# The order of the seven products in an FFN's second projection: 1, 5 | 7, 6, 2, 3 | 4 in place of 1 | 2 | 5, 6, 7, 3 | 4

## The chip, the cores and the metric

The kernel runs on one core of a Trainium2 chip. A core has five engines with instruction streams of their own: TensorE (PE; its weight loads are listed apart as PEld), VectorE (DVE), ScalarE (ACT), GpSimd (POOL) and SyncE (SP), and 16 DMA engines that serve transfers issued by SP, ACT and POOL. The metric is the device time of one execution in microseconds, the median over several runs.

## The reference

Two layers of an encoder over 512 tokens of width 1024. A layer is half an FFN, a mixer, and half an FFN; a last RMSNorm follows. All weights are float32.

```python
def swiglu(x, w_in, w_out):
    gu = x @ w_in
    g, u = jnp.split(gu, 2, axis=-1)
    return (jax.nn.silu(g) * u) @ w_out
...
    for l in range(L):
        x = x + 0.5 * swiglu(rms_norm(x, ffn1_norm[l]), ffn1_w_in[l], ffn1_w_out[l])
        x = x + mixer(rms_norm(x, mix_norm[l]), mix_w_in[l], mix_gate_bias[l], na_rpb[l],
                      na_w_out[l], f_w_out[l], mix_w_o[l])
        x = x + 0.5 * swiglu(rms_norm(x, ffn2_norm[l]), ffn2_w_in[l], ffn2_w_out[l])
    return rms_norm(x, final_norm)
```

So there are four FFNs. The change concerns the product with `w_out` (2816 x 1024) in each of them, called the second projection or the output stage below.

## The kernel before

**A matrix product as seven.** The kernel halves both operands of its large products in both directions and forms seven products of half size in place of eight (Strassen's scheme in Winograd's form). With a, b, c, d the quarters of the weight matrix (upper and lower left, upper and lower right) and A11, A12, A21, A22 those of the activations, the output stage computes

| product | activations | weights |
|---|---|---|
| 1 | A11 | -a |
| 2 | A21 | b |
| 5 | A11 - A12 | c + d |
| 6 | A11 - A12 + A22 | a + c + d |
| 7 | A12 - A22 | a + c |
| 3 | A22 | a + b + c + d |
| 4 | A21 - (A11 - A12 + A22) | d |

(with activations transposed, so that "rows" of the code's `part(h, j, c)` are h for the halves of the 2816 features and j for the halves of the tokens). Product 6 is added onto product 1 in PSUM, and product 4 onto product 7. Results go into x, which stays in SBUF as float32, by `update` (L817 to L820): one DVE instruction for each of the two 128-token blocks, x = x ± 0.25 · PSUM. Product 1 is read into x before product 6 is added to it, and once more after each further step that needs the sum.

**Chunks.** The 1408 features of a half are cut into three chunks of 3, 4 and 4 tiles of 128 (`CHUNK`, L47). A product of one chunk takes two granules of weights, of two 128 x 512 tiles each (in the first chunk the second granule has one tile); each granule is used for two blocks of tokens.

**Precision.** Each float32 operand is split into a high and a low part of a shorter type, and a tile of a product is three matmuls: high x high, high x low, low x high (L539, L540, L542; 128 x 512 each). The high part is an ACT copy, the low part a DVE subtraction. For weights these are L205 or L210 (`whi`) and L206 or L213 (`wlo`), with three buffers each; for activations L350 and L351 (`c1h`, `c1l` and so on, by the number of the product). The differences and sums of the activations are made in place by DVE (`comb`, L814).

**Weights.** `stage_items` (L220) writes out the whole list of granules in the order in which products use them; `strassen` (L226) makes the items of one product after the other. `Raw.load` (L150) issues a plain load from SP (L155) into one of nine `raw` tiles of an FFN stage, and, where the item has a `plus`, an accumulating DMA from POOL that adds a second block of weights onto the tile (L165). An item with `add` gets its second block by its own plain load and a DVE addition (`summed`, L182). An item with `then` gets a further block by an accumulating DMA once the item is split (L215); with `dma=True` (the last chunk of the last FFN) this takes the place of a DVE addition. Before, product 5 uses a tile d onto which c is accumulated, product 6 adds a to the same tile (DVE), product 3 adds b to it (DVE), and product 7 has a tile of its own, c with a accumulated. `Stream.next` (L334) lets the splits run two granules ahead of PE, and the loads eight items ahead in the instruction order (`FETCH`), as far as the nine tiles allow.

**Order.** In `stage_ffn` (L663) the second projection is a list `steps` (L822) of (product, chunk): product 1 for the three chunks, product 2 for the three, then 5, 6, 7, 3 of the first chunk, of the second and of the third, then product 4 for the three. `make(i)` builds the activation operand of step i, up to three steps ahead. The loop from L996 runs the products and puts around them, by step: the turned blocks of the FFN's inner activations (`joined`, after steps 3 and 5; the transposing DMA is L381), the updates of x, the squares for the next norm (ACT, L413), and the transposed quarters of x for the next stage (`nxt.quad`, L437 to L456: eight PE transposes L451, four ACT copies L454, one high part L455, one low part on DVE L456). Quarter (0, 0) is placed after step 6, which is product 5's first chunk; (1, 1) and (0, 1) after product 4's first chunk. In the last FFN (`late`) there are no quarters, and the final norm is woven in. 

**Banks.** The PSUM pool has eight tiles of 128 x 512 (L110). A product's output takes a pair. `ps` holds the pairs o1, o2, o5, o7, o3 while they are in use; product 6 uses o1, product 4 o7.

**Who decides the order.** Semaphores and the instruction order on each engine are set by the framework's scheduler: it takes the ready instruction that comes first in the program, by a model of the durations, so that DVE may run differences (L814) well ahead of the place where the code has them. Blocks under `manual_schedule` keep their order on the engines named.

Of the kernel before, what the change touches and what calls it, by code (L numbers as in the profile page):

```python
# [31 lines left out]
AHEAD = 2  # L32
ORDER = (1, 5, 2, 6, 7, 3, 4)
FIRST = (1, 2, 5, 6, 7, 3, 4)
FETCH = 8
UNIT = (0, 1, 4, 5)
KEYS = ((0, 6), (2, 5), (2, 4), (1, 6))
# [61 lines left out]
def encoder_kernel(  # L99
# [120 lines left out]
    def stage_items():  # L220
        items, st = [], 0

        def add(*a, **k):
            items.append(Item(*a, stage=st, **k))

        def strassen(s, name, idx, sizes, order, dma=False, behind=None, on_chip=False):  # L226
            def key(q, g):
                return (s, name(q), idx, g) if g < 2 else (s, "h" + q, idx, 0)

            r = {}  # L230
            for q, q2 in (("a", None), ("b", None), ("c", "a"), ("d", "c")):
                plus = q2 and not (on_chip and q == "c")
                r[q] = [Raw(key(q, g), n, key(q2, g) if plus else None) for g, n in enumerate(sizes)]
            d2 = [Raw(key("d", g), n) for g, n in enumerate(sizes)]
            at = [(m, g) for m in order for g in range(len(sizes))]
            if len(sizes) == 3:
                at.remove((2, 2))
                at.insert(at.index((7, 2)), (2, 2))
            for m, g in at:
                a, b, c, d = [r[q][g] for q in "abcd"]  # L240
                if m == 1:
                    add(a, neg=True)
                elif m == 2:
                    add(b)
                elif m == 3:
                    add(d, None if dma else b)
                elif m == 4:
                    add(d2[g])
                elif m == 5:
                    add(d)  # L250
                elif m == 6:
                    add(d, a, then=b.key if dma else None)
                else:
                    add(c, a if on_chip else None)
                for key in (behind or {}).get(m, ()) if g == len(sizes) - 1 else ():
                    add(Raw(key))

        def out_sizes(c):
            return (1024, 512) if c == 0 else (1024, 1024)

        def ffn(s):
            first = not items
            if first:
                for g in range(4):
                    add(Raw((s, "cl", g)), parts=2 if g < 2 else 1, pieces=2 if g == 0 else 1)
            for j in range(NB):
                order = (1, 2, 5, 6, 7, 3, 4) if first and j == 0 else (1, 5, 6, 2, 7, 3, 4)
                strassen(s, lambda q: q, j, (1024,) * (2 if first or j else 3), order)
            for order in ((1,), (2,), (5, 6, 7, 3), (4,)):
                for c in range(3):  # L270
                    summed = s == (L - 1, 2) and c == 2
                    strassen(s, lambda q: "o" + q, c, out_sizes(c), order, summed)

        for l in range(L):
            ffn((l, 1))
            st += 1
            s = (l, 0)
            two = (1024, 1024)
            qk = [(s, "qk", g) for g in range(8)]
            strassen(s, lambda q: "u" + q, 0, two, (1, 5, 6, 2, 3, 7, 4), True, behind={5: qk[0:1], 6: qk[1:2], 2: qk[2:3], 3: qk[3:4], 7: qk[4:5]})  # L280
            for key in qk[5:]:
                add(Raw(key))
            halves = [((s, "f", 2 * i), (s, "f", 2 * i + 1)) for i in range(2)]
            even = [Raw(t1, plus=t2) for t1, t2 in halves]
            for raw in even:
                add(raw)
            for raw, (_, t2) in zip(even, halves):
                add(raw, Raw(t2), twice=True)
            st += 1
            for g in range(2):  # L290
                add(Raw((s, "n", 0, g)))
            st += 1
            for i in range(2):
                strassen(s, lambda q: "g" + q, i, two, ORDER if i else FIRST, True, on_chip=False)
            for g in range(2):
                add(Raw((s, "n", 1, g)))
            strassen(s, lambda q: "w" + q, 0, two, ORDER, True)
            ffn((l, 2))
        return items
# [363 lines left out]
    def stage_ffn(norm, nxt, late):  # L663
# [140 lines left out]
        def part(h, j, c):  # L804
            return at[h, j, c][:, 0 : len(CHUNK[0][c]), :]
# [7 lines left out]
        def comb(dst, in0, in1, op):  # L813
            V.tensor_tensor(dst, in0, in1, op)  # L814
            return dst
# [3 lines left out]
                v = x[:, 2 * j + b, i * T : (i + 1) * T]  # L819
                V.scalar_tensor_tensor(v, ps[b], 0.25 * sign, v, ALU.mult, ALU.add)  # L820

        steps = []  # L822
        for c in range(3):
            steps.append((1, c, lambda c=c: part(0, 0, c)))
        for c in range(3):
            steps.append((2, c, lambda c=c: part(1, 0, c)))
        for c in range(3):
            steps.append((5, c, lambda c=c: comb(part(0, 0, c), part(0, 0, c), part(0, 1, c), ALU.subtract)))
            steps.append((6, c, lambda c=c: comb(part(0, 0, c), part(0, 0, c), part(1, 1, c), ALU.add)))
            steps.append((7, c, lambda c=c: comb(part(0, 1, c), part(0, 1, c), part(1, 1, c), ALU.subtract)))  # L830
            steps.append((3, c, lambda c=c: part(1, 1, c)))
        for c in range(3):
            steps.append((4, c, lambda c=c: fourth(c)))
        made = {}
        apart_by = set()

        def fourth(c):
            if c not in apart_by:
                comb(part(1, 0, c), part(1, 0, c), part(0, 0, c), ALU.subtract)
                apart_by.add(c)  # L840
            return part(1, 0, c)

        def make(i):
            if i < len(steps) and i not in made:
                m, c, f = steps[i]
                made[i] = hl(f(), c, f"c{m}")

        def two(settle):

# [143 lines left out]
        if late or nxt.mix:  # L993
            tc.keep_in_program_order(S.activation(small("sq", 1), ones, AF.Sqrt))
        ps = {}
        for i, (m, c, _) in enumerate(steps):  # L996
            make(i)
            if i:
                make(i + 1)
# [24 lines left out]
                    else:  # L1024
                        nxt.quad(0, 1)
            make(i + 2)
            if i == 6 and not late:
                nxt.quad(0, 0)
            if m == 4 and c == (0 if late else 1):
                update(ps[1], 1, 0, 1)  # L1030
# [7 lines left out]
            if m == 4 and c == 1 and late:  # L1038
                for _ in ready:
                    pass  # L1040
            if c < 2:
                continue
            if m == 1:
                update(ps[1], 0, 0, -1)
            elif m == 2:
                update(ps[2], 0, 0, 1)
                nxt.squares(0, 0)
            elif m == 5:
                update(ps[5], 0, 1, 1)
                update(ps[5], 1, 1, -1)  # L1050
            elif m == 6:
                if late:
                    make(i + 3)
                    fourth(2)
                update(ps[1], 1, 1, 1)
            elif m == 7:
                if late:
                    make(i + 3)
                update(ps[7], 1, 1, 1)
                nxt.squares(1, 1)  # L1060
            elif m == 3:
# [1191 lines left out]
```

## Time and profile before

| what | us |
|---|---|
| median of the runs | 1838.28 |
| lowest and highest run | 1833.59 and 1848.31 |
| the profiled execution | 1837.46 |
| its span, first to last instruction | 1835.7 |

The four output stages begin at 219.96, 811.81, 1130.85 and 1721.01 us of the span and take about 107 us each, three of them with the transposes for the next stage.

How to read the rows: the page's first part gives each engine's busy time, its share of the span and the number of instructions. The view of stretches gives, for each stretch of the span, its length, each engine's busy time with the number of instructions, the TensorE clock granted (1.00 is full speed), the DMA engines' mean busy share and GB/s. A timeline row has the start, the duration, the engine (a q behind it: its queue, which issues DMAs), the line, the operation, out<-in by the names of the program with shapes, and a count where equal instructions were merged; the idle time before it, and what ended it, stand in brackets. The page's list of DMA issues ends with the size and the median time from issue to landing.

### The profile page before, as it was taken

To read this page: it belongs to the slowest core of one execution; us is meant where nothing else is said; L and a number is where in the kernel's file an instruction comes from. 1 tells how busy PE (TensorE), PEld (TensorE's weight loads), DVE (VectorE), ACT (ScalarE), POOL (GpSimd) and SP (SyncE) were. 2 spreads that over 40 slices of the span, in tenths; PEclk is the share of its full clock that TensorE was granted. 3 is DMA by queue.
4 is the path that set the end of the run, shared out by engine and by line. 5 is a ranking of instruction groups with operands and counts; after the bars stand their busy time and mean duration, and the time that the engine had idled before them with its cause. 6 is when DMAs were issued, how large, how long until landed. Compare 5 with 4: busy or idle time off the path is not lost.

```text
span 1835.7 us, 24504 instructions
## 1 busy us (share of the span) xinstructions
PE 1823.8 (99%) x8766; PEld 1509.6 (82%) x8766; DVE 1607.2 (88%) x1952; ACT 1306.2 (71%) x1771; POOL 179.2 (10%) x219
## 2 busy tenths in 40 slices
PE   9999999999999999999999999999999999999998
PEld 7888888887878888888888888888888788888876
DVE  7878899878989988889998888998789899887898
ACT  6777875667576777787667777766776776777865
POOL 0001011110111010101010100101001111100010
PEclk9999999999999999999999999999999999999999
DMA  9898798963997789879878987998639876988795
GB/s 303 223 237 225 184 274 272 225 175 116 277 221 193 166 233 242 208 201 281 249 194 212 240 212 197 274 296 186 179 134 264 227 190 183 238 212 223 202 272 162
DMA packets 206387, 403.75 MB, mean 220 GB/s; under 512 B 108733, under 2 KB 108893, under 8 KB 206265
## 3 DMA queue, kind: packets, MB, share of 16 engines
q1 hardware_dynamic: 176536, 300.52, 51.0%
q0 software_dynamic: 29296, 101.12, 30.5%
q8 instruction: 69, 1.13, 0.3%
q10 hardware_dynamic: 432, 0.55, 0.1%
q14 instruction: 54, 0.43, 0.1%
HBM read 370.67 MB, written 2.11 MB: 203 GB/s over the span
## 4 chain that ended last, share of the span: by engine, by line
PE 89%; DVE 3%; DMA 3%; issue 2%; ACT 2%; POOL 0%; SPq 0%; DVEq 0%; ACTq 0%; POOLq 0%
PE A L539 10%; PE A L540 10%; PE A L542 10%; PE o L540 7%; PE o L539 7%; PE o L542 7%; PE B L542 5%; PE B L540 5%; PE B L539 5%; PE ps L344 3%; PE ps L345 3%; PE ps L346 2%; PE C L540 2%; PE C L539 2%; PE C L542 2%
## 5 line engine op out<-in xcount | busy, mean ns | idle before, releaser
L213 DVE TENSOR_TENSOR wlo<-raw,whi 128x1024 fp32r<-128x1024 f32 (+1 forms) x534 | 630.8, 1190 | 166.3 <-ACT whi L210 165.8
L210 ACT ACTIVATE whi<-raw 128x1024 fp32r<-128x1024 f32 (+1 forms) x534 | 546.2, 1033 | 265.4 <-DVE raw L182 70.7
L165 POOL DMA_DIRECT2D raw<-in_wst_dram x170 | 148.6, 900 | 1301.7 <-DMA raw<-in_wst_dram 467.6
L182 DVE TENSOR_TENSOR raw<-raw,raw 128x1024 f32<-128x1024 f32 (+1 forms) x148 | 176.1, 1190 | 2.0
L540 PE MATMUL A<-whi,xl 128*128 128x512 f32 x400 | 155.7, 389 | 0.0
L539 PE MATMUL A<-whi,xh 128*128 128x512 f32 x400 | 155.7, 389 | 0.0
L394 ACT ACTIVATE at<-zt 128x1024 uint16<-128x1024 uint16 (+2 forms) x96 | 110.2, 1165 | 12.0 <-DMA zt<-zs 12.0
L542 PE MATMUL A<-wlo,xh 128*128 128x512 f32 x400 | 115.0, 389 | 0.0
L205 ACT ACTIVATE whi<-raw 128x1024 fp32r<-128x1024 f32 (+1 forms) x83 | 85.6, 1036 | 38.7 <-issue 11.3
L206 DVE SCALAR_TENSOR_TENSOR wlo<-raw,whi 128x1024 fp32r<-128x1024 f32 (+1 forms) x83 | 98.6, 1192 | 11.5 <-ACT whi L205 11.5
L542 PEld LDWEIGHTS A<-wlo,xh 128*128 128x128 f32 x400 | 75.1, 188 | 15.6
L540 PEld LDWEIGHTS A<-whi,xl 128*128 128x128 f32 x400 | 75.1, 188 | 15.4
L539 PEld LDWEIGHTS A<-whi,xh 128*128 128x128 f32 x400 | 75.1, 188 | 15.4
L539 PE MATMUL B<-whi,xh 128*128 128x512 f32 x208 | 81.4, 391 | 1.2 <-ACT whi L210 1.1
L540 PE MATMUL B<-whi,xl 128*128 128x512 f32 x208 | 81.0, 390 | 0.0
L540 PE MATMUL C<-whi,xl 128*128 128x512 f32 x208 | 81.0, 389 | 0.0
L539 PE MATMUL C<-whi,xh 128*128 128x512 f32 x208 | 81.0, 389 | 0.0
L794 ACT ACTIVATE th<-sn,rh 128x512 f32<-128x512 f32 x80 | 54.9, 715 | 36.3 <-DVE sn L631 35.5
L375 ACT ACTIVATE zs<-th 128x1024 uint16<-128x1024 uint16 x80 | 79.5, 1043 | 0.9 <-DVE th L801 0.9
L626 ACT ACTIVATE sn<-A 128x512 f32<-128x512 f32 x104 | 59.0, 586 | 27.5 <-PE A L542 27.2
L542 PE MATMUL B<-wlo,xh 128*128 128x512 f32 x208 | 60.2, 391 | 0.2
L542 PE MATMUL C<-wlo,xh 128*128 128x512 f32 x208 | 60.1, 390 | 0.0
(451 smaller groups left out, 4618.7 us busy)
## 6 DMA issues: line engine op xcount, KB each, us to landing
raw<-in_wst_dram SPq DMA_DIRECT2D x468, 512.0 KB, 6.3
raw<-in_wst_dram POOLq DMA_DIRECT2D x180, 512.0 KB, 8.1
bm<-in_bias_dram SPq DMA_DIRECT2D x16, 512.0 KB, 6.2
raw<-in_wst_dram SPq DMA_DIRECT2D x30, 256.0 KB, 5.1
vs<-v SPq DMA_DIRECT2D x24, 128.0 KB, 5.8
x<-in_xin_dram SPq DMA_DIRECT2D x4, 512.0 KB, 10.2
raw<-in_wst_dram POOLq DMA_DIRECT2D x8, 256.0 KB, 8.4
dft<-in_dft_dram POOLq DMA_DIRECT2D x8, 256.0 KB, 6.7
```

The costliest lines, as they stand in the source:

```text
L165: G.dma_start(out=self.t, in_=wst[GRAN_AT[self.plus]][:, 0 : self.n], accum_op=ALU.add)
L182: V.tensor_tensor(self.raw.t, self.raw.t, self.add.t, ALU.add)
L205: S.activation(hi, t, AF.Copy, scale=-1.0)
L206: self.last = V.scalar_tensor_tensor(lo, t, -1.0, hi.bitcast(F32), ALU.mult, ALU.subtract)
L210: S.activation(hi[:, cs], t[:, cs], AF.Copy)
L213: self.last = V.tensor_tensor(lo[:, cs], t[:, cs], hi[:, cs].bitcast(F32), ALU.subtract)
L375: S.activation(s[:, h], words[:, h], AF.Copy)
L394: S.activation(to[:, w], t[:, w], AF.Copy)
L539: PE.matmul(ps, lh, rh, start=start, stop=False, skip_group_check=again)
L540: PE.matmul(ps, ll, rh, start=False, stop=False, skip_group_check=again)
L542: PE.matmul(ps, lh, rl, start=False, stop=stop, skip_group_check=again)
L626: last_snap[0] = S.activation(t[:, b, :], ps[b], AF.Copy)
```

## The change

The order becomes: products 1 and 5 chunk by chunk (first phase), then 7, 6, 2, 3 chunk by chunk (second phase), then product 4 (third phase). The order stands in one table, `OUT`, that both the list of weights and the list of steps follow.

The weight sums of product 6 and 3 are built on product 7's tile: c with a accumulated by DMA serves product 7, d is added to it by DVE for product 6 (with a plain load of d), and b, which product 2 has loaded in between, is added to it by DVE for product 3. In the last chunk of the last FFN b comes by an accumulating DMA after product 6's split, as before. Product 5's tile (d with c accumulated) is used by product 5 alone. A plain load of a and one of b per granule go, and one of d comes.

In the loop: product 5's two updates of x come apart, the first after its last chunk, the second after product 6's first chunk; the transposed quarter (0, 0) goes from product 5's first chunk to product 3's last; the updates of 7 and 6 follow the new order. The number `i` of the steps at which `joined` runs (3 and 5) is the same, so these now follow product 5 of the second and third chunk.

```diff
+OUT = ((1, 5), (7, 6, 2, 3), (4,))
...
-        def strassen(s, name, idx, sizes, order, dma=False, behind=None, on_chip=False):
+        def strassen(s, name, idx, sizes, order, dma=False, behind=None, from_c=False):
...
                 elif m == 2:
                     add(b)
+                elif from_c and m in (6, 3):
+                    add(c, d2[g] if m == 6 else None if dma else b, then=b.key if dma and m == 6 else None)
                 elif m == 3:
                     add(d, None if dma else b)
...
-                    add(c, a if on_chip else None)
+                    add(c)
...
-            for order in ((1,), (2,), (5, 6, 7, 3), (4,)):
+            for order in OUT:
                 for c in range(3):
                     summed = s == (L - 1, 2) and c == 2
-                    strassen(s, lambda q: "o" + q, c, out_sizes(c), order, summed)
+                    strassen(s, lambda q: "o" + q, c, out_sizes(c), order, summed, from_c=True)
...
-        steps = []
-        for c in range(3):
-            steps.append((1, c, lambda c=c: part(0, 0, c)))
...
+        steps = [(m, c) for order in OUT for c in range(3) for m in order]
...
-            if i == 6 and not late:
+            if (m, c) == (3, 2) and not late:
                 nxt.quad(0, 0)
...
+            if (m, c) == (5, 2):
+                update(ps[5], 0, 1, 1)
+            if (m, c) == (6, 0):
+                update(ps[5], 1, 1, -1)
             if c < 2:
                 continue
...
             elif m == 5:
-                update(ps[5], 0, 1, 1)
-                update(ps[5], 1, 1, -1)
+                pass
+            elif m == 7:
+                if late:
+                    make(i + 3)
+                update(ps[7], 1, 1, 1)
             elif m == 6:
                 if late:
                     make(i + 3)
                     fourth(2)
                 update(ps[1], 1, 1, 1)
-            elif m == 7:
-                if late:
-                    make(i + 3)
-                update(ps[7], 1, 1, 1)
                 nxt.squares(1, 1)
```

More of the change, by code (lines that the diff above doesn't have):

```diff
@@ L231, in strassen @@
             for q, q2 in (("a", None), ("b", None), ("c", "a"), ("d", "c")):
-                plus = q2 and not (on_chip and q == "c")
-                r[q] = [Raw(key(q, g), n, key(q2, g) if plus else None) for g, n in enumerate(sizes)]
+                r[q] = [Raw(key(q, g), n, key(q2, g) if q2 else None) for g, n in enumerate(sizes)]
             d2 = [Raw(key("d", g), n) for g, n in enumerate(sizes)]
@@ L293, in stage_items @@
             for i in range(2):
-                strassen(s, lambda q: "g" + q, i, two, ORDER if i else FIRST, True, on_chip=False)
+                strassen(s, lambda q: "g" + q, i, two, ORDER if i else FIRST, True)
             for g in range(2):
@@ L820, in update @@
                 V.scalar_tensor_tensor(v, ps[b], 0.25 * sign, v, ALU.mult, ALU.add)
-        steps = []
-        for c in range(3):
-            steps.append((1, c, lambda c=c: part(0, 0, c)))
[L825 to L833, printed above, removed]
+        operand = {
+            1: lambda c: part(0, 0, c),
+            2: lambda c: part(1, 0, c),
+            5: lambda c: comb(part(0, 0, c), part(0, 0, c), part(0, 1, c), ALU.subtract),
+            7: lambda c: comb(part(0, 1, c), part(0, 1, c), part(1, 1, c), ALU.subtract),
+            6: lambda c: comb(part(0, 0, c), part(0, 0, c), part(1, 1, c), ALU.add),
+            3: lambda c: part(1, 1, c),
+            4: lambda c: fourth(c),
+        }
+        steps = [(m, c) for order in OUT for c in range(3) for m in order]
         made = {}
@@ L844, in make @@
             if i < len(steps) and i not in made:
-                m, c, f = steps[i]
-                made[i] = hl(f(), c, f"c{m}")
+                m, c = steps[i]
+                made[i] = hl(operand[m](c), c, f"c{m}")
         def two(settle):
@@ L995, in stage_ffn @@
         ps = {}
-        for i, (m, c, _) in enumerate(steps):
+        for i, (m, c) in enumerate(steps):
             make(i)
```

## The prediction

> **What bounds the kernel now.** I read the page first, then what PE waits for, then PE's timeline in the output stages, then all four output stages cut into their phases, and DVE last, as the busiest engine beside PE. The page:
>
> ```profile
> span 1835.7 us, 24504 instructions
> PE 1823.8 (99%) x8766; PEld 1509.6 (82%) x8766; DVE 1607.2 (88%) x1952; ACT 1306.2 (71%) x1771; POOL 179.2 (10%) x219
> raw<-in_wst_dram SPq DMA_DIRECT2D x468, 512.0 KB, 6.3
> raw<-in_wst_dram POOLq DMA_DIRECT2D x180, 512.0 KB, 8.1
> ```
>
> PE is busy for 99% of the span. Since matmuls overlap, that alone doesn't say that PE is full; the spacing of their starts does. PE's timeline where the first FFN's output stage begins:
>
> ```profile
> 219.96 0.39 PE L539 MATMUL o<-whi,c1h 128*128 128x512 f32 x1
> 220.19 0.39 PE L540 MATMUL o<-whi,c1l 128*128 128x512 f32 x1
> 220.41 0.39 PE L539 MATMUL o<-whi,c1h 128*128 128x512 f32 x1
> 220.64 0.39 PE L540 MATMUL o<-whi,c1l 128*128 128x512 f32 x1
> ```
>
> The reader is to see the starts, not the durations: three steps take 0.68 us, 0.227 us each. The stages cut into products 1 and 2, products 5, 6, 7, 3, and product 4 (the first FFN's three rows, then the middle row of the second and third FFN, then the last FFN's first two):
>
> ```profile
> core 0: us, PE busy (x) PEld busy (x) DVE busy (x) ACT busy (x) POOL busy (x), PEclk, DMA share, GB/s
> 219.96:249.91 29.95, 29.95 (x133) 24.71 (x132) 29.12 (x31) 26.47 (x29) 3.48 (x4) 1.00 0.96 235
> 249.91:310.85 60.94, 60.94 (x273) 50.30 (x272) 60.42 (x62) 38.15 (x49) 7.48 (x9) 1.00 0.93 283
> 310.85:327.00 16.15, 16.15 (x81) 13.57 (x80) 14.20 (x18) 11.35 (x19) 1.71 (x2) 1.00 0.82 235
> ...
> 841.73:902.51 60.78, 60.78 (x273) 50.39 (x272) 60.42 (x62) 38.09 (x49) 6.90 (x8) 1.00 0.92 271
> ...
> 1160.80:1221.71 60.91, 60.91 (x273) 50.31 (x272) 60.40 (x62) 38.14 (x49) 6.91 (x8) 1.00 0.95 282
> ...
> 1721.01:1750.96 29.95, 29.95 (x133) 24.70 (x132) 29.12 (x31) 26.48 (x29) 4.35 (x5) 1.00 0.85 228
> 1750.96:1812.35 61.39, 60.68 (x265) 49.34 (x264) 57.65 (x60) 36.30 (x43) 7.80 (x9) 1.00 0.93 261
> ```
>
> Products 1 and 2 are 132 matmuls: 132 x 0.2267 = 29.93 us, against 29.95 measured. There is nothing to take out of them. Products 5, 6, 7, 3 are 264 matmuls, 59.85 us; the first three FFNs add eight transposes and take 60.8 to 60.9; the last FFN has no transposes there and takes 61.39, so 1.54 us of it is a stall. It is the only sizeable one of the output stages, and its cause stands in the chain of waits at that place:
>
> ```profile
> 1760.16 9.46 DMA raw<-in_wst_dram
> ...
> 1769.72 1.07 ACT whi L210
> ...
> 1770.81 1.24 DVE wlo L213
> ```
>
> The accumulating DMA that adds c onto d for product 5, second chunk, landed 9.46 us after its issue; high half, low half and then PE came behind it. DVE is the second engine to watch: 29.12 + 60.42 + 14.20 = 103.7 us busy in the 107.0 us of the first stage, so it has 3.3 us spare and still doesn't hold PE up.
>
> **The change part by part.** The sum is made against the profiled execution: 1837.46 us, of which 1835.7 is the span and 1.8 lies around it. The median of the runs shown is 1838.28, 0.8 above it.
>
> PE's work: the same seven products over the same three chunks, the same transposes. 0 us.
>
> Loads on SP. Before, one granule (two k-tiles of a quadrant) takes seven plain loads: a, b, d, a, c, b, d. After, it takes six: a, d, c, d, b, d. The last chunk of the last FFN stays at six. With 24 granules in four stages, 22 loads go: 18 of 512 KB, 4 of 256 KB, 10.5 MB. DMA moves 283 GB/s in the 5, 6, 7, 3 phase without PE waiting for it, apart from the stall above, so fewer loads give 0 beyond that.
>
> Accumulating DMAs on POOL: two per granule as before (c onto d for product 5, a onto c for product 7), but product 5's now fall into the first phase. What they need: 6.3 us for the load and 8.1 for the addition, 14.4 together. What they have: in a phase where each granule takes one tile, the nine weight tiles reach nine granules of 12 x 0.227 = 2.72 us ahead, 24.5 us; even with the 9.46 us of the bad case, that leaves 8 us. The two transposing DMAs of the last block stand in SP's queue there as they did before; behind them come the loads of the second phase, in the same places as before:
>
> ```profile
> 202.76 20.17 SPq L155 DMA_DIRECT2D raw<-in_wst_dram  x9
> 223.04 6.77 SPq L381 DMA_TRANSPOSE zt<-zs  x2
> 229.90 77.02 SPq L155 DMA_DIRECT2D raw<-in_wst_dram  x36
> ...
> 235.16 1.75 POOL L165 DMA_DIRECT2D raw<-in_wst_dram  x2 [54.07 <-DVE wlo L213]
> ```
>
> POOL has issued nothing for 54 us when the first addition for product 5 goes out; after, those go out some 30 us earlier, into that idle time. In the second phase c is held from product 7 to product 3 but d no longer, six tiles per eight granules in place of eight, so the tiles reach further. Bounds: a late addition costs 0 to 1.5 us a stage (the last FFN's stall is the nearest row); I take 0. The stall that is there now belongs to the crowded phase; I take it away: -1.5, bounds -1.5 and 0.
>
> DVE's work: the same instructions. The additions of weights stay at two a granule: c + d and c + b on product 7's tile in place of d + a and d + b. What moves is the activation side, L814: product 5's three differences must be made in the first phase.
>
> ```profile
> 219.96:249.91 29.95, 7.38 (x7) 1.00 0.96 235
> 249.91:310.85 60.94, 5.80 (x5) 1.00 0.93 283
> ```
>
> This is L814 alone. DVE pulls seven of the twelve into the first phase already, 1.05 us each. After, three are product 5's, and four more are ready in time (7's and 6's for the first two chunks): seven again. 0; the upper bound is in the first rival. The weight splits of product 5 take the place of those of product 2, one for one; product 2's update and its squares of the norm go one phase later, where ACT is busy for 38 of 61 us. In the last FFN product 4's operand for the second chunk is made one product later, with two products still to go: 0.
>
> A new wait: the kernel keeps eight PSUM tiles, two for a product's pair. In the second phase o1, o7, o2 and o3 take all eight, and o3's pair must come from o5, once both updates of x have read it (L820). How late DVE takes such updates:
>
> ```profile
> 250.34 1.28 DVE L820 SCALAR_TENSOR_TENSOR x<-o,x 128x512 f32<-128x512 f32 x2
> ...
> 296.36 2.48 DVE L820 SCALAR_TENSOR_TENSOR x<-o,x 128x512 f32<-128x512 f32 x4
> ...
> 303.29 1.28 DVE L820 SCALAR_TENSOR_TENSOR x<-o,x 128x512 f32<-128x512 f32 x2
> ...
> 308.76 1.28 DVE L820 SCALAR_TENSOR_TENSOR x<-o,x 128x512 f32<-128x512 f32 x2
> ...
> 312.83 2.47 DVE L820 SCALAR_TENSOR_TENSOR x<-o,x 128x512 f32<-128x512 f32 x4
> ```
>
> The first follows product 2's end (249.91) by 0.4 us; the last follows product 3's end (310.85) by 2.0 and is done after 4.5. Counting back from 310.85 by 24 x 0.227 = 5.44 us, the products 5, 6 and 7 that the three between belong to ended at 294.5, 300.0 and 305.4. For o3, product 5 ends, then 7, 6 and 2 of the first chunk run (3 x 18 x 0.227 = 12.2 us) before PE needs the pair. The second update is queued behind product 6, 8.2 us in; with the slowest of these delays it ends at 12.7, 0.5 us late. Behind the waiting product 3 stands all of PE. Bounds 0 and 0.5 us a stage, 2 in all; I take 0, since the nearest row, the update at the phase's edge, starts after 0.4. In return product 4's wait for o7 eases: product 7 of the last chunk now ends 16 us before product 4 instead of 5.4, and its update ended at 310.0 for 310.85.
>
> The transposed quarter (0, 0) of the next norm moves from product 5's first chunk to behind product 3's last:
>
> ```profile
> 254.00 1.03 PE L451 MATMUL tr<-ident,x 128*128 128x128 f32 x8
> ...
> 314.94 1.91 PE L451 MATMUL tr<-ident,x 128*128 128x128 f32 x16
> ...
> 254.98 1.55 ACT L454 ACTIVATE xr<-tr,gn 128x256 f32<-128x256 f32 x4
> ...
> 257.14 1.07 ACT L455 ACTIVATE xh<-xr 128x1024 fp32r<-128x1024 f32 x1
> ```
>
> Its eight transposes cost PE the same wherever they stand. They now need product 2's update 5.4 us after product 2 ends; the updates above end 1.7 to 4.7 us after theirs. ACT's copies and high half, 2.6 us, go into a phase in which it is busy for 11.35 of 16.15. DVE's one low half of it, 1.1 us, can push the update that the transposes at 314.94 need: those of 312.83 ended at 315.3, and the second eight start at 315.8, 0.8 later after the change. Bounds 0 and 0.5 us in each of three stages (the last FFN has none); I take 0.25, +0.7 in all.
>
> Sum: 1837.46 - 1.5 + 0.7 = 1836.7 us: no change that can be measured.
>
> **The rivals.** A, slower: DVE becomes the bound in the second phase. Place: products 7 and 6 of the first two chunks. If the four early differences can't be pulled forward (6's must wait until product 5's halves are made from the same tile), DVE has 60.42 + 14.20 + 4 x 1.05 = 78.8 us to do in the 77.1 us of phases two and three, 1.7 us a stage. From that on PE waits one for one: 4 x 1.7 = 7, and with the bank wait's 2 on top of the sum: 1846. For over 1% it would take 4.6 us in each stage, more than its 3.3 us of spare time and the two granules that it works ahead can hide: 18.4 us, 1856. For it: DVE at 97%. Against: its total is unchanged.
>
> B, the change does nothing: the additions are as late as before somewhere else, and the last FFN's stall stays: 1838.2. For it: product 7's additions now open the second phase, in the place of product 5's. Against: nothing stalls in that place before.
>
> C, faster: PE isn't full. Its weight loads fill only 82% of the span; if that were its degree of use, up to 18%, 330 us, would be open, and a smoother mix of DVE and DMA could let PE run closer together. Against: those loads fill 24.71 of 29.95 us, 82% as well, in the first phase, whose matmuls start 0.227 us apart without a gap; so 82% is what a full PE shows with these matmuls. What the output stages' one stall leaves to win ends at 1836, and over 1% faster would be 1819, for which no row has room. This reading is a rule of the Trainium skill ("Perfetto Trace Analysis", section Identifying the Most-Contended Engine): matmul busy time doesn't show how near TensorE is to its peak, the busy share of the weight loads does. By that rule there would be headroom; by the spacing of the starts here there is none.
>
> **How the numbers follow.** About 1% either way, 18 us, is what a measurement of this kernel can tell from no change: the three runs lie between 1833.59 and 1848.31. Chances: the forecast 0.55, B 0.2, A 0.2, of it 0.04 beyond 1%; C beyond 1% 0.01; the remaining 0.04 are small shifts in the mixers, whose instructions are ordered anew too, within 1%. So faster 0.01, same 0.95, slower 0.04. The range reaches from 1832 (the lowest run shown less the 1.5 us) to 1846 (A).
>
> **What would show it right or wrong.** Right: starts 0.227 us apart through both phases; 61.39 falls to about 59.9 in the last FFN for 264 matmuls; SP's 468 loads are 450 and the 256 KB ones 26; DVE's busy time in a stage stays 103.7. A shows as PE waiting for low halves in the second phase, the bank wait as product 3's first matmul of the first chunk waiting for an L820 at its start, and the quarter as a gap ahead of transposes at the third phase's edge. A gap of over 1 us in every stage would make the forecast wrong.

## The result, and the profile after

| what | before, us | after, us |
|---|---|---|
| median of six runs each | 1837.11 | 1890.02 |
| lowest and highest run | 1833.59 and 1848.31 | 1883.28 and 1894.94 |
| the profiled execution | 1837.46 | 1891.28 |
| its span | 1835.7 | 1889.5 |

The changed kernel is slower: the ratio is 1.027, with a 95% interval of 1.0235 to 1.031. The forecast was no change. The spans differ by 53.8 us, and this is what has to be found. First the page of the kernel after: span, busy times, the group of ACT's copies of the turned blocks, one group of PE, and three rows of DMA issues.

```profile
span 1889.5 us, 24470 instructions
PE 1833.3 (97%) x8766; PEld 1515.5 (80%) x8766; DVE 1607.6 (85%) x1952; ACT 1308.0 (69%) x1771; POOL 179.0 (9%) x219
...
L396 ACT ACTIVATE at<-zt 128x1024 uint16<-128x1024 uint16 (+2 forms) x96 | 110.9, 1165 | 71.9 <-DMA zt<-zs 71.9
...
L541 PE MATMUL o<-whi,c1h 128*128 128x512 f32 x88 | 38.8, 440 | 43.2 <-ACT whi L206 43.2
...
raw<-in_wst_dram SPq DMA_DIRECT2D x450, 512.0 KB, 5.8
raw<-in_wst_dram POOLq DMA_DIRECT2D x180, 512.0 KB, 7.9
...
raw<-in_wst_dram SPq DMA_DIRECT2D x26, 256.0 KB, 13.4
```

The work is what was foretold: 8766 matmuls, DVE busy for 1607.6 us against 1607.2, 450 and 26 loads on SP. What is new stands behind the last bar of two groups. PE was idle for 43.2 us ahead of product 1's matmuls (`c1h`), for high halves made by ACT. And ACT was idle for 71.9 us ahead of its copies of the turned blocks, for the transposing DMA zt<-zs; the same row of the kernel before has 12.0:

```profile
L394 ACT ACTIVATE at<-zt 128x1024 uint16<-128x1024 uint16 (+2 forms) x96 | 110.2, 1165 | 12.0 <-DMA zt<-zs 12.0
```

PE's waits by releaser, after, with total, number and the longest:

```profile
PE o L541 <- ACT whi L206: 43.2, 4, 14.8
```

Four waits, one in each output stage. The view of stretches, cut at the new phases (first and second phase of the first FFN, the first phases of the next three, the second of the last), shows that nearly all of the loss lies there:

```profile
core 0: us, PE busy (x) PEld busy (x) DVE busy (x) ACT busy (x) POOL busy (x), PEclk, DMA share, GB/s
220.13:261.21 41.08, 32.05 (x133) 26.05 (x132) 28.21 (x30) 26.02 (x28) 5.19 (x6) 0.88 1.08 223
261.21:321.44 60.23, 60.23 (x265) 49.36 (x264) 60.23 (x63) 36.25 (x44) 3.78 (x5) 1.00 0.68 214
823.12:870.67 47.55, 32.75 (x133) 26.56 (x132) 29.36 (x31) 24.98 (x26) 5.18 (x6) 0.82 1.02 195
1159.90:1199.61 39.71, 32.16 (x134) 26.09 (x133) 28.32 (x30) 25.90 (x28) 5.18 (x6) 0.91 1.07 228
1762.09:1806.66 44.57, 32.73 (x134) 26.53 (x132) 28.89 (x30) 26.06 (x28) 5.20 (x6) 0.85 1.05 211
1806.66:1866.50 59.84, 59.84 (x266) 49.55 (x264) 59.76 (x63) 37.36 (x46) 3.46 (x4) 1.00 0.65 184
```

A first phase is still 132 matmuls, 29.93 us. The four take 41.08, 47.55, 39.71 and 44.57: 11.2, 17.6, 9.8 and 14.6 too long, 53.2 of the 53.8 us. The rest is the last FFN's stall that went (1.5 us won) and some 2 us lost between the third and the fourth output stage. The second phases run without a gap of half a microsecond.

Now one such place, in the first FFN. ACT's timeline, then PE's (what ended the idle time stands in brackets):

```profile
233.47 1.07 ACT L206 ACTIVATE whi<-raw 128x1024 fp32r<-128x1024 f32 x1
247.59 2.53 ACT L396 ACTIVATE at<-zt 128x1024 uint16<-128x1024 uint16 x2 [13.05 <-DMA zt<-zs]
249.99 1.03 ACT L206 ACTIVATE whi<-raw 128x1024 fp32r<-128x1024 f32 x1
```

```profile
251.08 0.80 PE L541 MATMUL o<-whi,c1h 128*128 128x512 f32 x1 [9.03 <-ACT whi L206]
251.67 0.63 PE L542 MATMUL o<-whi,c1l 128*128 128x512 f32 x1
252.10 0.63 PE L541 MATMUL o<-whi,c1h 128*128 128x512 f32 x1
```

ACT runs its instructions in order. The two copies of the last turned block (`joined` after step 3, which takes the two blocks in reverse order) wait 13.05 us for the transposing DMA; behind them stands the high half of product 1's last granule, and PE waits 9.03 us for that. Once the copies are done the split starts at once (249.99), with no wait for its weights. Here are the DMA issues of SP and then of POOL; the span of an issue is that of the queue instruction, not of the transfer:

```profile
223.82 5.10 SPq L383 DMA_TRANSPOSE zt<-zs  x1
...
229.63 5.56 SPq L383 DMA_TRANSPOSE zt<-zs  x1
```

```profile
228.32 0.86 POOL L166 DMA_DIRECT2D raw<-in_wst_dram  x1 [9.81 <-DVE at L816]
229.70 0.86 POOL L166 DMA_DIRECT2D raw<-in_wst_dram  x1 [0.52 <-DMA raw<-in_wst_dram]
235.95 0.87 POOL L166 DMA_DIRECT2D raw<-in_wst_dram  x1 [5.38 <-DVE c1l L353]
```

SP issues the second transposing DMA at 229.63, nearly as before (228.08). But POOL now issues additions at 228.32, 229.70 and 235.95, where before it had issued nothing for 54 us until 235.16. By the packets of the trace, this transposing DMA ran from 234.70 to 246.89, 12.2 us; between its first and last packet, 602 KB (here and below of 1000 bytes) of the accumulating DMAs moved. Its first packet also came later, 5.1 us after the issue in place of 1.3. In the other three stages it took 16.6, 11.4 and 15.4 us with 999, 684 and 963 KB of them. In the kernel before, the transposing DMAs at these places took 2.5 to 4.0 us, each with 0 KB of accumulating traffic. The two together do not merely share the DMA engines; for a while both almost stop. After, in stretches (columns as above):

```profile
222.00:230.00 8.00, 8.00 (x37) 6.63 (x36) 8.00 (x9) 7.97 (x11) 1.16 (x2) 1.00 1.11 271
230.00:236.00 6.00, 6.00 (x29) 4.95 (x28) 6.00 (x7) 4.54 (x5) 0.62 (x2) 1.00 1.17 240
236.00:242.00 6.00, 6.00 (x27) 4.69 (x25) 2.19 (x2) 0.00 (x0) 0.81 (x1) 1.00 1.13 127
242.00:247.00 5.00, 0.05 (x1) 0.00 (x0) 0.00 (x0) 0.00 (x0) 0.00 (x0) 0.78 1.10 39
247.00:256.00 9.00, 4.92 (x14) 3.92 (x15) 4.94 (x5) 8.40 (x9) 0.87 (x1) 0.56 1.04 314
251.00:255.00 4.00, 3.92 (x9) 3.15 (x10) 3.94 (x4) 4.00 (x6) 0.59 (x1) 0.50 1.00 315
```

The reader is to set the last two columns side by side: from 242 to 247 the DMA engines count as fully busy (1.10) and move 39 GB/s, a seventh of the 271 at 222 to 230; of the packets that begin there, 17 are of additions and 38 of the transposing DMA's 2048. As soon as the transposing DMA is done, 314 GB/s follow. For comparison the same place of the kernel before, while its two transposing DMAs run with no additions:

```profile
225.00:232.00 7.00, 7.00 (x33) 5.70 (x32) 7.00 (x7) 6.97 (x9) 0.00 (x0) 1.00 1.25 184
225.00:228.00 3.00, 3.00 (x15) 2.49 (x14) 3.00 (x4) 2.97 (x5) 0.00 (x0) 1.00 1.18 104
```

The share is above 1 there too, but 184 GB/s move. The second row is the start of the first: a transposing DMA alone has a slow stretch as well, of 3 us, and 245 GB/s from 228 to 232 behind it. The wait has a second price, in the last row of the kernel after: after 9 us of idling PE's granted clock is 0.50 for about 4 us, and the matmuls start 0.43 us apart (251.67, 252.10) in place of 0.227. Some ten matmuls at 0.2 us more are 2 us a stage: 9.0 + 2.0 make the first FFN's 11.2.

### The profile page after: what moved, and what is told of

It is laid out like the page before. It is cut to its first block, busy times and chain, and to the rows that moved or that the text cites. A ratio compares the mean times of both kernels' runs of the same rounds, so it can differ in the third digit from the quotient of the medians.

```text
span 1889.5 us, 24470 instructions
## 1 busy us (share of the span) xinstructions
PE 1833.3 (97%) x8766; PEld 1515.5 (80%) x8766; DVE 1607.6 (85%) x1952; ACT 1308.0 (69%) x1771; POOL 179.0 (9%) x219
## 5 line engine op out<-in xcount | busy, mean ns | idle before, releaser
L396 ACT ACTIVATE at<-zt 128x1024 uint16<-128x1024 uint16 (+2 forms) x96 | 110.9, 1165 | 71.9 <-DMA zt<-zs 71.9
L541 PEld LDWEIGHTS A<-whi,xh 128*128 128x128 f32 x400 | 75.1, 188 | 15.4
L541 PE MATMUL o<-whi,c1h 128*128 128x512 f32 x88 | 38.8, 440 | 43.2 <-ACT whi L206 43.2
```

Of the source, the lines that this page charges most:

```text
L396: S.activation(to[:, w], t[:, w], AF.Copy)
L541: PE.matmul(ps, lh, rh, start=start, stop=False, skip_group_check=again)
```

## The experiments

The theory at the start: product 5's additions fall on the last block's transposing DMAs, these take four times as long or more, ACT's copies wait for them, and product 1's weights wait behind the copies. Its rivals: that ACT's order alone is to blame; that any traffic issued by POOL at that time would do it; that something else in the new order does it (DVE, the PSUM pairs, the sums on product 7's tile). Ratios stand to runs of the kernel before on the same chip.

**Copies later in ACT's order.** The turned blocks are joined four steps later; the transposing DMAs stay where they are.

```diff
-            if i == 3:
+            if i == 7:
                 turned.reverse()
                 joined()
-            if i == 5:
+            if i == 9:
                 joined()
```

> The changed kernel with ACT's copies of the last block's turned words put two products into the second phase (after product 6 and after product 3 of the first chunk) in place of behind product 5's second and third chunk. Theory 1 (accumulating DMAs in flight slow the last transposing DMA, and ACT's copies that wait for it hold up product 1's weight split behind them in ACT's queue): the transposing DMA stays slow, 15 to 20 us from issue to landing, but ACT no longer waits for it, PE's four waits for whi of 8 to 15 us are gone, and the time is 1836 to 1839. Rival 2 (product 1's third chunk has its own late weights or operands in the new order): the four waits stay, about 1890.

Measured: 1888.33 us, ratio 1.023 (1.020 to 1.0265). The gain that was expected did not come, and the time is the one that rival 2 named. What speaks against that rival is where PE waits: the four waits at product 1 are gone. The copies no longer hold ACT up, but the last blocks' transposing DMAs still took 15.7 to 22.3 us, and now weights of the next products land late. PE's waits, one of ACT's rows, and a stretch of this kernel:

```profile
PE o L541 <- ACT whi L211: 35.9, 9, 8.0
```

```profile
249.21 1.06 ACT L211 ACTIVATE whi<-raw 128x1024 fp32r<-128x1024 f32 x1 [8.54 <-DMA raw<-in_wst_dram]
```

```profile
236.00:257.00 21.00, 16.72 (x62) 12.78 (x60) 9.77 (x10) 4.35 (x5) 0.87 (x1) 0.84 1.12 57
```

So ACT's order only decides which operand is late first. For 21 us the DMA engines moved 57 GB/s, and ACT, then PE, waited for weights: the cause is in the transfers.

**Product 5 without c.** Product 5 takes d alone in the output stages, by a plain load; the addition of c is left out.

```diff
                 elif m == 5:
-                    add(d)
+                    add(d2[g] if from_c else d)
```

> The changed kernel without c in product 5's weights in the output stages (product 5 uses d alone), so no accumulating DMA falls into the first phase. Theory 1: the last transposing DMA lands 4 to 6 us after its issue as before the change, no wait of PE over 1 us, 1835 to 1838. Rival 1 (the bytes moved in the first phase slow it, whatever moves them): the same here, since the bytes go too. Rival 2: the waits stay, about 1890.

Measured: one run, 1833.61 us, beside 1842.03 for the kernel before. The transposing DMAs of the output stages took 2.3 to 4.1 us, and PE's longest wait in the whole span was 1.2 us, at the start. The order, the steps, the PSUM pairs and the sums on product 7's tile all stayed, and the loss is gone: none of them alone is the cause.

**The same bytes from POOL, not accumulated.** POOL loads d over d, plainly; product 5 again works with d alone.

```diff
-            G.dma_start(out=self.t, in_=wst[GRAN_AT[self.plus]][:, 0 : self.n], accum_op=ALU.add)
+            src = wst[GRAN_AT[self.plus]][:, 0 : self.n]
+            if self.over:
+                G.dma_start(out=self.t, in_=wst[GRAN_AT[self.key]][:, 0 : self.n])
+            else:
+                G.dma_start(out=self.t, in_=src, accum_op=ALU.add)
```

> The changed kernel with product 5's accumulating DMA in the output stages replaced by a plain DMA of the same size from the same POOL queue, which writes d over d (product 5 uses d alone). Theory 1a (it is the accumulation that collides with the transposing DMA): as without it, 1835 to 1840. Theory 1b (any such DMA from POOL's queue beside the transposing one) and rival 1 (bytes): the transposing DMA takes 11 us and more between its first and last packet again, PE waits 5 to 15 us in each stage, 1870 to 1890.

Measured: one run, 1851.88 us, between the two expected ranges. The transposing DMAs of the output stages took 2.4 to 8.5 us, the longer ones with 299 to 680 KB of POOL's traffic beside them. PE's and ACT's waits:

```profile
PE o L547 <- ACT whi L211: 5.6, 4, 2.4
```

```profile
ACT at L402 <- DMA zt<-zs: 34.9, 9, 7.1
```

The wait is at the same place and costs an eighth (5.6 us in place of 43.2). So plain traffic from POOL beside a transposing DMA costs something too. Whether it costs less than the accumulating kind at like amounts is not settled: 8.5 us with 680 KB stand against 11.4 with 684 KB in the kernel after, but 5.9 with 299 KB against 5.8 with 311 KB of additions in a mixer of the kernel before.

**Additions put into the old order.** The kernel before, but product 2's weights are a added onto b by an accumulating DMA in place of b alone, so that additions fall into its first phase as well.

```diff
-            for order in ((1,), (2,), (5, 6, 7, 3), (4,)):
+            for order in ((1,), ("2+",), (5, 6, 7, 3), (4,)):
...
+                elif m == "2+":
+                    add(Raw(key("b", g), sizes[g], key("a", g)))
```

> The kernel before, in its own order, with one thing added: product 2's weights in the output stages get a by an accumulating DMA (product 2 uses a + b), so that accumulating DMAs are in flight in the first two phases. Theory 1: the last transposing DMA takes over 10 us between its first and last packet, ACT's copies of the turned words wait for it, and PE waits 5 to 15 us in each of the four stages: 1865 to 1890. Rival 2 (the order of the products is the cause): no new wait, 1836 to 1842.

Measured: one run, 1938.41 us, worse than expected. The first of the two transposing DMAs of a last block took 18.3 to 27.8 us, with 1257 to 1540 KB of accumulating traffic beside it. PE's waits, and three stretches at the first FFN:

```profile
PE o L541 <- ACT whi L210: 87.3, 4, 26.3
```

```profile
230.00:242.00 12.00, 12.00 (x55) 9.85 (x53) 8.83 (x10) 4.63 (x6) 0.87 (x1) 1.00 1.30 65
242.00:251.00 9.00, 0.37 (x2) 0.00 (x0) 0.00 (x0) 0.00 (x0) 0.00 (x0) 0.70 1.32 89
251.00:264.00 13.00, 0.00 (x0) 0.00 (x0) 0.00 (x0) 0.00 (x0) 0.00 (x0) 0.50 1.24 80
```

The new order isn't needed for the loss. Additions beside the transposing DMAs are enough here: DMA share 1.2 to 1.3 at 65 to 89 GB/s. This edit also adds additions that the kernel before doesn't have, so its size is not that of the change.

**The two halves of the change, one at a time.** First the new sums without the move: product 7's tile serves 6 and 3, product 5 stays in the second phase (its updates and quarter (0, 0) go with it).

```diff
-OUT = ((1, 5), (7, 6, 2, 3), (4,))
+OUT = ((1,), (2,), (5, 7, 6, 3), (4,))
```

> One part of the change alone: the order 1 | 2 | 5, 7, 6, 3 | 4 with the weight sums of products 6 and 3 on product 7's tile; product 5 and the transposed quarter stay where they were before. Theory 1: accumulating DMAs are in flight with the last transposing DMA only where product 5 is moved, so the transposing DMA lands after 4 to 6 us, there is no new wait of PE, and the time is 1834 to 1839. If the sums on product 7's tile were part of the cause: over 1850.

Then the move with the old sums on d's tile:

```diff
-OUT = ((1, 5), (7, 6, 2, 3), (4,))
+OUT = ((1, 5), (6, 7, 2, 3), (4,))
...
-                    strassen(s, lambda q: "o" + q, c, out_sizes(c), order, summed, from_c=True)
+                    strassen(s, lambda q: "o" + q, c, out_sizes(c), order, summed)
```

> The other part alone: product 5 in the first phase, and the weight sums as before, on product 5's kind of tile (c accumulated onto d again for product 6, then a, then b): 1, 5 | 6, 7, 2, 3 | 4. Theory 1: the same collision as in the changed kernel, the last transposing DMA 11 us and more between its packets, PE waits of 5 to 15 us in each stage, 1870 to 1900. If the sums on product 7's tile were the cause: 1836 to 1845.

Measured: the sums alone 1850.72 us, ratio 1.005 (1.0023 to 1.0076), above the expected range and just over the 1850 that were to speak for the sums as part of the cause; the move alone, one run, 1917.68, above its expected range too. PE's waits, the move alone first:

```profile
PE o L541 <- ACT whi L206: 48.0, 4, 14.7
PE o L542 <- DVE c6l L353: 5.8, 3, 2.1
```

```profile
PE B L541 <- ACT whi L211: 8.0, 3, 7.6
PE o L544 <- DVE wlo L214: 3.9, 5, 0.9
PE o L541 <- ACT whi L211: 2.8, 1, 2.8
```

With the move the four waits are there, with transposing DMAs of 11.6 to 19.2 us; with the sums alone they are not (2.4 to 3.9 us). So the move carries most of the loss. The new sums are not free either: some 0.9 us a stage for low halves at product 6, a wait of 2.8 us in the last FFN for weights that landed late, and in the profiled execution one wait of 7.6 us in the first mixer. There a transposing DMA took 12.3 us with 713 KB of accumulating traffic beside it (5.8 us and 311 KB before): the same meeting at another place, which this edit doesn't touch.

**The additions held back.** The kernel after; a 64-byte DMA on POOL reads the last turned block, and the additions for product 5's third chunk and product 7's first follow it in POOL's order. Every transfer is kept, of the same kind; only their meeting is gone. (The kernel has the same device, `released`, in the first block of three of its FFNs.)

```diff
+        seen = dp.tile([16], F32, tag="seen", name=nm("seen"))
+        to = bass.AP(tensor=seen.tensor, offset=seen.offset, ap=[[16, 1], [1, 16]])
+        landed = G.dma_start(out=to, in_=turned[-1][0][0:1, 1, 0, 0:32].bitcast(F32)).ins
+        held.update({(stage, q, c, g): landed for q, c in (("od", 2), ("oc", 0)) for g in range(2)})
```

> The changed kernel with the accumulating DMAs of product 5's third chunk and product 7's first chunk held in POOL's queue until the last transposing DMA has landed (a 64-byte DMA that reads its tile stands ahead of them). Same bytes, same kinds of DMA, only not at the same time. Theory 1: the transposing DMA lands within 9 us of its issue, each addition within 10 us; product 5's third chunk gets its weights up to 5 us late in a stage: 1838 to 1858. Rival 1 (it is the bytes moved in that stretch): the additions and the loads are as slow as in the changed kernel, 1880 or more.

Measured: 1860.9 us, ratio 1.010 (1.006 to 1.0145), 3 us above the expected range and well below the 1880 of rival 1. POOL's timeline, the stretch that moved 127 and 39 GB/s in the kernel after, and PE's longest waits:

```profile
236.64 0.53 POOL L995 DMA_DIRECT2D seen<-zt  x1 [18.26 <-DMA zt<-zs]
237.25 3.54 POOL L166 DMA_DIRECT2D raw<-in_wst_dram  x4
```

```profile
236.00:242.00 6.00, 6.00 (x28) 4.95 (x28) 4.60 (x5) 4.44 (x4) 4.07 (x5) 1.00 0.97 300
242.00:247.00 5.00, 3.44 (x16) 2.54 (x15) 1.76 (x2) 1.74 (x2) 0.00 (x0) 1.00 1.05 243
```

```profile
PE B L541 <- ACT whi L211: 7.2, 3, 6.2
PE o L541 <- ACT whi L211: 7.0, 8, 2.3
PE o L544 <- DVE wlo L214: 5.5, 7, 0.8
```

This is the run that decides. The transposing DMAs of the output stages are back at 2.2 to 3.8 us, the additions go out behind them at 300 and 243 GB/s, and of the 2.7% about 1.7 are gone. What is left, 3 to 6 us a stage, are mostly the additions that now come late (issued together, the four of the first FFN landed after 7.9 to 15.0 us, not within 10; PE waited 2.3 us at most at product 5's third chunk), and again one wait in a mixer (6.2 us; its transposing DMA took 12.1 us with 799 KB beside it).

**The additions on DVE.** If the accumulating DMAs are the trouble, DVE can add c to d from two plain loads: once for product 5's third chunk alone, once for all of it.

```diff
+                elif m == 5 and from_c and idx == 2:
+                    add(d2[g], Raw(key("c", g), sizes[g]))
```

> The changed kernel with c added to product 5's weights of the third chunk by DVE, from a plain load of its own, in place of the accumulating DMA (two more loads from SP and two more DVE additions a stage, two accumulating DMAs fewer). Theory 1: what is left in flight beside the transposing DMAs is the end of the second chunk's additions, the last transposing DMA lands within 7 us, no wait of PE over 2 us, DVE's 2.3 us more a stage are hidden or cost up to 1 us: 1834 to 1842. Rival 1 (bytes): as slow as the changed kernel, 1880 or more.

```diff
+                elif m == 5 and from_c:
+                    add(d2[g], Raw(key("c", g), sizes[g]))
```

> The changed kernel with c added to all of product 5's weights in the output stages by DVE, from plain loads (six more loads from SP and six more DVE additions a stage; no accumulating DMA in the first phase, the same bytes). Theory 1: the last block's two transposing DMAs land 4 to 7 us after their issue and nothing waits for them; what is left is DVE, with 6.3 us more work in a stage that had 3.3 us spare: 0 to 4 us a stage, 1838 to 1856. If the time in the changed kernel came from the bytes of the first phase, it would stay over 1880.

Measured: 1854.87 us for the third chunk, ratio 1.0065 (1.004 to 1.009); 1872.75 for all, ratio 1.016 (1.011 to 1.0215). Both are above what was expected. In both the transposing DMAs of the output stages took 2.2 to 4.4 us; the four long waits are gone. With the third chunk alone no wait of PE in the whole span is longer than 2.7 us; matmuls a little late remain in the first two output stages (some 4.6 and 2.5 us in sum) and at the start of the first mixer (7.6). With all of product 5's additions DVE is busy for 1632.8 us, 25 more than after, and PE waits for the splits of activations:

```profile
PE o L543 <- ACT c6h L354: 5.9, 4, 1.8
PE o L544 <- DVE c7l L355: 5.1, 5, 1.6
```

The output stages are 5 to 8 us longer than before. That fits DVE as the bound: the additions had been on the DMA for a reason. No version that computes the whole was faster than the kernel before.

**What the runs say together.** Length of a transposing DMA, first to last packet, against the accumulating traffic that moved in between:

| accumulating traffic beside it | length, us | seen in (plain loads from POOL left aside) |
|---|---|---|
| 0 to 61 KB | 2.0 to 4.8 | most transposing DMAs of all kernels; in the last blocks before, with the additions held back, on DVE or left out |
| 78 to 172 KB | 3.0 to 5.1 | mostly mixers |
| 242 to 471 KB | 3.9 to 14.0 | mixers; the second transposing DMAs with the additions in the old order; three in earlier blocks of an FFN |
| 602 to 1016 KB | 11.4 to 22.3 | after, joined later, the move alone; mixers with the new sums alone and with the additions held back |
| 1257 to 1540 KB | 18.3 to 27.8 | additions in the old order |

The table alone proves little, since a transposing DMA that takes longer also has more moving beside it, and its third row scatters. Part of the scatter has an order in it. The three in earlier blocks (sums alone, all on DVE, additions in the old order) took only 4.5 to 4.7 us with 434 to 471 KB, and 211 to 223 GB/s moved. There an addition was in full flow when the transposing DMA's first packet came (365 to 389 KB in the 2 us before), and no further one began. In the fourth row less was in flight before (at most 172 KB), and additions began while the transposing DMA ran. So the amount is not all that counts; no run changes this order alone. What carries the verdict is that the meeting was taken away with all else kept (held back) and brought about in the old order, and the length followed both times. How much of it is due to the accumulating, rather than to POOL's traffic as such, rests on one run with plain loads, which came at other times than the additions. Why the two hinder each other inside the DMA engines, no record here shows. Also open: why a transposing DMA of the first mixer meets more additions in some kernels (713 and 799 KB) than in before (311) or after (242), and so what part of the 0.5% of the sums alone is due to the new sums themselves.

## Why the prediction was wrong

**The step that failed** is the one on the accumulating DMAs: "a late addition costs 0 to 1.5 us a stage ... I take 0", for additions that "go out some 30 us earlier, into that idle time". The bounds covered only an addition that comes too late for its own product. The lead times behind them (6.3 us for a load, 8.1 for an addition, 24.5 at hand) were medians over the whole kernel before, where hardly any addition meets a transposing DMA. The paragraph named the right neighbour, the two transposing DMAs that "stand in SP's queue there as they did before", and treated it as a matter of order on a queue. They did stand there as before. What had changed was what ran beside them: the trace of before showed POOL idle for 54 us around them and hence no accumulating traffic during them, so for this place it had no row for the two together, and the cost should have been left open upwards. It was 53.2 us in place of 0: four waits of 43.2 us, and the rest mostly the slow clock behind them.

The kernel before did hold two hints. In its first mixer a transposing DMA met 311 KB of additions and took 5.8 us, the longest in that kernel, and the addition issued at 525.50 landed only after 11.27 us, on the chain that ended last:

```profile
525.50 11.27 DMA raw<-in_wst_dram
```

And `released` (L750) holds two additions back in the first block of three FFNs until a transposing DMA has landed; POOL waits 59.7 us in all for that (L754). The code doesn't say why, and the prediction used neither.

**The neighbour's customers** were missing as well. Behind a late turned block stood ACT's copies, and behind these, in order, the weight split that PE needed next: 13.05 us late at ACT, 9.03 at PE. The prediction followed the additions to product 5, not the transposing DMAs to ACT.

**What held.** The last FFN's stall went: 61.39 became 59.84 for the same 264 matmuls, 1.55 for the 1.54 forecast. The second phases run at the matmuls' own pace; 60.23 in the first FFN is 264 matmuls and small delays of 0.4 in all. DVE's total stayed, PE waited in the second phase neither for low halves nor, at product 3, for its PSUM pair, and no gap showed at quarter (0, 0), so the +0.7 taken for it was not spent. SP's loads fell as counted.

**The rivals.** A, DVE as the bound, is not what happened, but a loss that fits its mechanism came as soon as DVE got 25 us more. B is refuted, since the stall went. C's reading of the weight loads' share finds no support: 49.55 of 59.84 us is 83% in a phase without a gap. The check named at the end, "a gap of over 1 us in every stage", is what came true.

How close the forecast would have been without the meeting is shown by product 5 without c: 1833.61 in one run with that part of the work left out. With c added and product 5 in the first phase, the best was the one with DVE's additions for the third chunk, 0.65% above before.

## What to carry to other kernels

When a transfer is moved, list what else is in flight at its new time, of which kind, and who waits for those transfers, not only whether its own queue is idle and its own lead is long enough. Look for the one place in the whole trace where the two already meet, here a mixer, and read the price there. A pair of transfers that the trace never shows together has no row, and "hidden" is then a guess; a short run that brings the two together tells its price. Read DMA share and GB/s together: busy engines that move little for longer than a transfer takes alone point to transfers that hinder each other.

## What the runs showed of the hardware

In the last blocks, accumulating DMAs that began while a transposing DMA ran and that transposing DMA slowed each other and the plain loads: 39 to 89 GB/s at a DMA share of 1.1 to 1.3, against 184 for transposing DMAs without additions and 243 to 300 for the additions behind them. It is not so at every meeting: three with an addition already in full flow took 4.5 to 4.7 us at 211 to 223 GB/s. An addition of the kernel after landed 15.8 us after its issue (235.95 to 251.79, against a median of 7.9), but so late came the fourth of those held back, too, so this number alone doesn't show it.

A wait of PE can cost more than its length: after 9 us the clock was 0.50 for about 4 us. The Trainium skill ("TensorE: Matmul & The Clock Gate", section What's actually happening) states that the array falls to half its clock after an idle window of about 3.4 us and comes back after about as long a busy one. The trace agrees in the half clock (251 to 255: 0.50, starts 0.43 us apart; from 255.75 on 0.23 us apart) and roughly in the times: by its clock records, in the four stages, the clock fell 2.7 to 5.1 us after the end of the last matmul and came back 3.9 to 5.5 us after the start of the next one.
